# Attention outputs turned into rows by VectorE block transposes and a way through DRAM, and a changed entry into attention

## The chip, the cores and the metric

One core of a Trainium2 chip runs the kernel. The metric is the device time of one execution in microseconds. Of the kernel before, two runs were timed, 1617.72 and 1619.03 us, median 1618.38 us. A further execution was profiled.

## What is computed

The reference is one layer of a gated backbone over 1024 latent tokens and 256 context tokens, width 1024, all in float32. The normalised input goes through one wide projection into two branches, gated linear attention (GLA, four heads) and differential attention (eight heads of width 128), which are projected, gated, summed and projected again. The part around the change is differential attention and the first half of what follows it:

```python
a = jax.nn.softmax(s1, axis=-1) - lam * jax.nn.softmax(s2, axis=-1)
return jnp.einsum('bhqk,bhkv->bhqv', a.astype(v.dtype), v)
...
b = merge_heads(rms_norm(o_diff) * diff_gain * (1 - lam_init)) * jax.nn.silu(diff_gate)
y = jax.nn.sigmoid(m_gla) * (a @ w_br_gla) + jax.nn.sigmoid(m_diff) * (b @ w_br_diff)
```

The norm is over a token's 128 values in a head, so it needs the attention output with tokens along partitions. The product with w_br_diff contracts over those values and needs them along partitions again.

## The kernel before, in words

**Numbers and engines.** A float32 product is made of three float32r products of high and low parts. The high part is a rounding copy (ACT, or POOL from a copy), the low part a subtraction (DVE or POOL). TensorE (PE) also does all 128x128 transposes, by line 375; line 349 issues all other matmuls.

**Order.** The program is written by a scheduler in its own text. Tasks are Python generators. The class Driver (from line 59) keeps a modelled time for each engine and for the DMA queue, and resumes a task when what it yielded is due. `On(t, engine)` resumes it when that engine is about to come free, `AtPE(t)` when PE's modelled time reaches t, and any other time up to 1 us early (AHEAD, line 70). Of tasks due together, the one with the lowest `prio` number issues first. Each engine then runs its instructions strictly in the order in which they were issued, waiting on semaphores where the model was wrong. Driver.dma (lines 134 to 145) models a transfer: 0.45 us of issue on one shared queue, 0.6 us, the bytes at 360 GB/s, 1.8 us to the landing. All DMAs are issued by SP, one queue, in order: an issue that waits holds up all those behind it. `acq` and `rel` (lines 330 and 338) count the buffers of a tag; the table TAGS (line 235) gives each tag its pool and number.

**Stages.** Until about 900 us: projections, GLA. Then attention, 64 units (8 heads of 8 query tiles of 128). For a unit, PE makes two score rows of 1280 in the five PSUM banks of tile "s5", DVE takes maxima, ACT the exponentials, DVE the difference, PE ten transposes through the two "b1" banks, and ACT, POOL and DVE split them into "at". For a pair of units PE multiplies by the values into a "b1" bank (30 matmuls, `att_av`, line 2067). An order list (`att_order`, line 1914) fixes how scores, transposes and products of different units follow each other. Between them, `fill` (line 2193) puts independent matmuls into the one bank "mb": the rest of the gate projection, then the GLA output projection, 18 weight tiles in two halves each, with weights converted by `conv` (line 2210) from "raw" into "wt". From about 1458 us: the projection of attention's output in seven block products (`diff`), then the last projection.

**The pair's end**, `att_fin` (line 2142), runs once for each of 32 pairs (head hd, pair pr). It loads the gate values g (128 tokens x 2 x 128). ACT copies the product po to `ot`, whose 128 partitions are values and whose 256 columns are tokens. PE transposes its halves into pt, a "b1" bank (line 2160). ACT squares and sums each half, DVE multiplies pt by g, DVE and POOL make the inverse root, DVE scales into `oo`, PE transposes back into pb (line 2183), ACT copies that, and a DMA stores it in d_bT, from where `diff` loads it. The task holds one of two "fin" slots from before the products of `att_av` until the store is issued, and up to five "b1k" buffers are shared by such tasks.

**The entry.** GLA's last step for a head and group of 256 tokens is `post` (line 1795): it transposes the gated output through a PSUM tile "tp" (line 1816), splits it and stores it. `to_gla` (line 1277) waits for the last of them and closes GLA's PSUM pool with "gs", "go" and "gt"; `to_b` (line 2582) then waits for "mm" and "tp", closes their pool, opens the pools of "mb" and "s5" in that place and lets attention and fill begin. `half_tile` (line 2245) waits for its weight tile's event, which `conv` sets after one ACT copy and one DVE subtraction of 128x1024.

Of the kernel before, what the change touches and what calls it, by code (L numbers as in the profile page):

```python
# [20 lines left out]
P = 128  # L21
# [4 lines left out]
NK = D // P  # L26
# [206 lines left out]
class Hybrid:  # L233
# [6 lines left out]
        w=("sbA", 18), p=("sbA", 5), pl=("sbA", 4), rope=("sbA", 1),  # L240
# [6 lines left out]
        gsm=("sbA2", 8), gbi=("sbA2", 2), fresh=("sbA2", 1),  # L247

        wt=("sbW", 4), ft=("sbW", 2), aq=("sbG", 4), xa=("sbG", 4), vv=("sbB", 3),
        e5=("sbF", 6), at4=("sbB", 6), at2=("sbB", 2), ac=("sbB", 2), b1k=("sbB", 5), fin=(None, 2),  # L250

        ya=("sbC", 8), yb=("sbC", 8), yc=("sbD", 8), yf=("sbK", 8), yg=("sbG", 8), sf=("sbC", 2), o=("sbC", 4), wr=("sbD", 4), yd=("sbD", 4),

# [150 lines left out]
    def scratch(self):  # L404
        d = self.dram
        self.d_q = [d(f"d_q{h}", [P, S]) for h in range(4)]
        self.d_k = [d(f"d_k{h}", [P, T]) for h in range(4)]
        self.d_la = [[d(f"d_la{r}{h}", [P, T]) for h in range(4)] for r in range(2)]
        self.d_v = [d(f"d_v{c}", [T, 512]) for c in range(2)]
        self.d_gg = [d(f"d_gg{c}", [S, 512]) for c in range(2)]  # L410
        self.d_dg = [d(f"d_dg{c}", [S, 512]) for c in range(2)]
        self.d_dv = [[d(f"d_dv{j}{c}", [T, 512]) for c in range(2)] for j in range(2)]
        self.d_qT = [d(f"d_qT{c}", [4, P, 2, S]) for c in range(2)]
        self.d_kT = [[d(f"d_kT{j}{c}", [4, P, T]) for c in range(2)] for j in range(2)]
        self.d_aT = [[d(f"d_aT{j}{h}", [2, P, S]) for h in range(4)] for j in range(2)]
        self.d_bT = [d(f"d_bT{i}", [P, S]) for i in range(8)]
        self.d_m = [[d(f"d_m{j}{i}", [P, S]) for i in range(8)] for j in range(2)]
        self.d_pre = {n: d(f"d_pre_{n}", [P, 4, 512]) for n in ("w11", "w21", "w22", "t1", "t2", "t3", "t4")}
        self.ev_pre = {(n, kk): Event() for n in self.d_pre for kk in range(4)}
        self.ev_gbt = Event()  # L420
        self.d_ps = {n: d(f"d_ps_{n}", [4, P, 512]) for n in ("s1", "s2", "s3", "s4")}
        self.ev_ps = {(n, k): Event() for n in self.d_ps for k in range(4)}
        self.d_y = [d(f"d_y{i}", [P, S]) for i in range(8)]


# [1073 lines left out]
    def gla_head(self, h):  # L1499


        nc, d = self.nc, self.d
# [292 lines left out]
        def post(g, po):  # L1795

            r0 = (g - 1) * 256
            for x in range(2):
                yield self.ev_st["gg", h // 2, 2 * g - 2 + x]
            yield from self.acq("gp")  # L1800
            gt = self.t("gp", [P, 2, 256])
            self.dma(gt, self.d_gg[h // 2][r0:r0 + 256, cols].rearrange("(c p) e -> p c e", p=P))
            ss = self.t("sm", [P, 2])
            for x in range(2):
                en = self.act.activation(self.gj, po[:, x], AF.Square, accum_out=ss[:, x:x + 1])
            yield en
            self.pool.tensor_scalar(ss, ss, 1.0 / 256, EPS, ALU.mult, ALU.add)
            self.pool.tensor_tensor(ss, ss, self.nhalf[:, 0:2], ALU.pow)
            yield self.d.when(ss, gt)
            for x in range(2):  # L1810
                e = self.dve.scalar_tensor_tensor(gt[:, x], po[:, x], ss[:, x:x + 1], gt[:, x], ALU.mult, ALU.mult)
            self.rel("go", e)
            yield AtPE(e)
            yield from self.acq("tp")
            yield from self.acq("pl", 2)
            pt = self.t("tp", [P, 2, 2, P])
            for c in range(2):
                for x in range(2):
                    e = self.tr(pt[:, x, c], gt[:, c, x * P:(x + 1) * P])
            self.rel("gp", e)  # L1820
            yield e
            hi = self.t("pl", [P, 2, 2 * P], F32R)
            lo = self.t("pl", [P, 2, 2 * P], F32R)
            e = yield from self.split(pt.rearrange("p x c t -> p x (c t)"), hi, lo)
            self.rel("tp", e)
            self.store([(self.d_aT[j][h][:, :, r0:r0 + 256].rearrange("x p t -> p x t"), x) for j, x in
                        enumerate((hi, lo))], ("pl", 2))
            self.aT_left -= 1
            if self.aT_left == 0:
                d.set(self.ev_gla)  # L1830
# [311 lines left out]
    def att_fin(self, hd, pr, po, zs):  # L2142

        nc, d = self.nc, self.d
        yield from self.acq("b1k", 2)
        g = self.t("b1k", [P, 2, P])
        self.dma(g, self.d_dg[hd // 4][pr * 256:(pr + 1) * 256, (hd % 4) * P:(hd % 4 + 1) * P].rearrange(
            "(c p) e -> p c e", p=P))
        ot = self.t("b1k", [P, 256])
        e = self.act.activation(ot, po, AF.Copy)  # L2150
        self.rel(self.PO, e)
        z2 = self.t("sm", [P, 2])
        for x in range(2):
            self.dve.tensor_scalar(z2[:, x:x + 1], zs[x][:, 0:1], zs[x][:, 0:1], EPS, ALU.mult, ALU.mult)
        yield AtPE(e)
        yield from self.acq("b1k")
        yield from self.acq("b1")
        pt = self.t("b1", [P, 2, P])
        for x in range(2):
            e = self.tr(pt[:, x], ot[:, x * P:(x + 1) * P])  # L2160
        self.rel("b1k", e)
        yield On(e, "ACT")
# [4 lines left out]
        yield d.on("DVE", pt, g)  # L2167
        e2 = self.dve.tensor_tensor(g, pt, g, ALU.mult)
        self.rel("b1", max(e, e2))
        yield On(e, "DVE")  # L2170
        for x in range(2):
            self.dve.tensor_scalar(ss[:, x:x + 1], ss[:, x:x + 1], 1.0 / P, z2[:, x:x + 1], ALU.mult, ALU.add)
        yield d.on("POOL", ss)
        yield On(self.pool.tensor_tensor(ss, ss, self.nhalf[:, 0:2], ALU.pow), "DVE")
        for x in range(2):
            e = self.dve.tensor_scalar(oo[:, x], g[:, x], ss[:, x:x + 1], None, ALU.mult)
        self.rel("b1k", e)
        yield AtPE(e)
        yield from self.acq("b1k")
        yield from self.acq("b1")  # L2180
        pb = self.t("b1", [P, 2, P])
        for x in range(2):
            e = self.tr(pb[:, x], oo[:, x])
        self.rel("b1k", e)
        yield On(e, "ACT")
        bb = self.t("b1k", [P, 2, P])
        self.rel("b1", self.act.activation(bb, pb, AF.Copy))
        self.store([(self.d_bT[hd][:, pr * 256:(pr + 1) * 256], bb.rearrange("p x t -> p (x t)"))],
                   ("b1k", 1), ("fin", 1), ev=self.ev_bp[hd, pr])
        if (hd, pr) == (7, 3):  # L2190
            self.d.set(self.ev_att)

    def fill(self):


        d, a = self.d, self.a
        todo = [(0, s, self.win, C_MG + s * P) for s in range(self.fill_from, 16)] + \
               [(1, s, a["w_br_gla"][0], s * P) for s in range(8)]
        evs = [[Event()] for _ in todo]
        ws = {}  # L2200

        def load():
            for n, (kind, _, src, o) in enumerate(todo):
                yield from self.acq("raw")
                raw = self.t("raw", [P, NK, P])
                yield self.dma(raw, src[:, o:o + P].rearrange("(k p) c -> p k c", p=P))
                d.spawn(conv(n, raw), 0.0, prio=3)
            d.set(self.ev_loaded)

        def conv(n, raw):  # L2210
            yield self.ev_b2
            yield from self.acq("wt", 2)
            if n == len(todo) - 1:
                d.set(self.ev_conv)
            hi = self.t("wt", [P, NK, P], F32R)
            lo = self.t("wt", [P, NK, P], F32R)
            yield d.on("ACT", raw)
            self.act.activation(hi, raw, AF.Copy)
            yield d.on("DVE", hi)
            e = self.dve.tensor_tensor(lo, raw, hi.bitcast(F32), ALU.subtract)  # L2220
            self.rel("raw", e)
            ws[n] = (hi, lo)
            d.set(evs[n][0], e)

        yield self.wlast
        d.spawn(load(), prio=3)
        yield self.ev_b

# [381 lines left out]
    def phase_c(self):  # L2610
        a, d = self.a, self.d
# [3 lines left out]
        def to_c():  # L2615
# [10 lines left out]
            self.open("sbD")  # L2626
            d.set(self.ev_c1)
            yield self.ev_att
            yield from self.idle("b1", "b1k", "vv", "at4", "at2", "ac")
            self.close("psB1", "sbB")  # L2630
            self.open("sbC", "psD")
            d.set(self.ev_c2)
# [173 lines left out]
```

## Time and profile before

| | us |
|---|---|
| median of the two runs | 1618.38 |
| the profiled execution | 1616.59 |
| its span, first to last instruction | 1614.9 |
| DMA: share of 16 engines' time, queue of SP | 63.7% |
| ACT busy / DVE busy / POOL busy | 836.2 / 1223.5 / 634.2 |

The profile page gives busy time for each engine (PE matmuls, PEld weight loads, DVE = VectorE, ACT = ScalarE, POOL = GpSimd, SP = the queue of DMAs). Matmuls overlap in their pipeline, so a matmul's duration in the profile is longer than the time from its start to the next one's start; the second is its place in PE's row. Groups are named by tiles, out<-in. A wait is put down to the instruction that released it.

### The profile page before, as it was taken

To read this page: it belongs to the slowest core of one execution; us is meant where nothing else is said; L and a number is where in the kernel's file an instruction comes from. 1 tells how busy PE (TensorE), PEld (TensorE's weight loads), DVE (VectorE), ACT (ScalarE), POOL (GpSimd) and SP (SyncE) were. 2 spreads that over 40 slices of the span, in tenths; PEclk is the share of its full clock that TensorE was granted. 3 is DMA by queue.
4 is the path that set the end of the run, shared out by engine and by line. 5 is a ranking of instruction groups with operands and counts; after the bars stand their busy time and mean duration, and the time that the engine had idled before them with its cause. 6 is when DMAs were issued, how large, how long until landed. Compare 5 with 4: busy or idle time off the path is not lost.

```text
span 1614.9 us, 24351 instructions
## 1 busy us (share of the span) xinstructions
PE 1590.6 (98%) x8229; PEld 1328.0 (82%) x8229; DVE 1223.5 (76%) x2117; ACT 836.2 (52%) x1719; POOL 634.2 (39%) x663
## 2 busy tenths in 40 slices
PE   7999999999999999999999999999999999999999
PEld 3788888888888888888888788888888888888887
DVE  4787945576877779767677688878788888889994
ACT  4776523445343454655435466665665656656331
POOL 1500000001325667535464256656765666560000
PEclk9999999999999999999999999999999999999999
DMA  8576896998778467564645944545587555348662
GB/s 310 199 256 242 330 305 230 343 328 297 275 246 267 123 198 233 163 212 122 185 118 165 251 116 121 151 128 150 151 265 218 158 136 151 112 152 280 210 206 100
DMA packets 259565, 331.16 MB, mean 205 GB/s; under 512 B 22600, under 2 KB 160752, under 8 KB 259440
## 3 DMA queue, kind: packets, MB, share of 16 engines
q1 hardware_dynamic: 259440, 329.60, 63.7%
q8 instruction: 65, 1.06, 0.3%
q14 instruction: 60, 0.49, 0.1%
HBM read 225.20 MB, written 104.33 MB: 204 GB/s over the span
## 4 chain that ended last, share of the span: by engine, by line
PE 91%; DVE 4%; ACT 1%; DMA 1%; POOL 1%; issue 1%; SPq 0%; ACTq 0%; DVEq 0%; POOLq 0%
PE mm L349 31%; PE mb L349 11%; PE s L349 8%; PE mc L349 7%; PE b L349 6%; PE tp L349 6%; PE gt L349 5%; PE b L375 4%; PE gs L349 4%; PE go L349 4%; PE mz L349 2%; PE tp L375 2%; DVE sm L201 1%; POOL at L201 1%; DMA w<-in_w_ada 1%
## 5 line engine op out<-in xcount | busy, mean ns | idle before, releaser
L349 PE MATMUL mm<-w,h 128*128 128x512 f32 x912 | 231.0, 400 | 0.0
L349 PE MATMUL mb<-h,wt 128*128 128x512 f32 x840 | 222.8, 400 | 0.0
L201 DVE TENSOR_REDUCE sm<-s 128x1 f32<-128x1024 f32 (+1 forms) x192 | 193.3, 1037 | 16.4 <-PE s L349 9.9
L201 ACT ACTIVATE e<-s,sm 128x1280 f32<-128x1280 f32 x128 | 169.3, 1328 | 57.7 <-DVE sm L201 54.5
L349 PEld LDWEIGHTS mm<-w,h 128*128 128x128 f32 x912 | 167.4, 188 | 32.7
L201 POOL TENSOR_TENSOR at<-ac,at 128x512 fp32r<-128x512 f32 x128 | 186.6, 1458 | 10.7
L349 PEld LDWEIGHTS mb<-h,wt 128*128 128x128 f32 x840 | 151.4, 188 | 28.7 <-DVE ft L201 0.3
L201 POOL TENSOR_SCALAR at<-ac 128x512 fp32r<-128x512 f32 x128 | 98.4, 768 | 192.2 <-ACT ac L201 191.7
L349 PE MATMUL s<-hk,aq 128*128 128x512 f32 x744 | 169.2, 364 | 1.9 <-ACT e L201 1.8
L349 PE MATMUL mm<-h,w 128*128 128x512 f32 x672 | 168.2, 400 | 1.1 <-DVE h L201 1.1
L349 PEld LDWEIGHTS mm<-h,w 128*128 128x128 f32 x672 | 123.7, 188 | 26.5 <-DVE h L201 1.6
L201 DVE TENSOR_TENSOR w<-raw,w 128x512 fp32r<-128x512 f32 x128 | 95.7, 764 | 53.4 <-ACT w L201 51.2
L349 PEld LDWEIGHTS s<-hk,aq 128*128 128x128 f32 x744 | 117.6, 189 | 19.1 <-ACT e L201 4.3
L349 PE MATMUL b<-at,vv 128*128 128x256 f32 x960 | 130.1, 287 | 1.1 <-ACT ac L201 0.8
L349 PEld LDWEIGHTS b<-at,vv 128*128 128x128 f32 x960 | 119.5, 191 | 2.8 <-ACT ac L201 1.0
L201 ACT ACTIVATE w<-raw 128x512 fp32r<-128x512 f32 x128 | 78.1, 626 | 84.0 <-PE tp L349 23.8
L201 DVE SCALAR_TENSOR_TENSOR e<-e,sm,e 128x1280 f32<-128x1280 f32 x64 | 118.3, 1849 | 0.9
L201 ACT ACTIVATE ac<-b 128x512 f32<-128x512 f32 x122 | 72.4, 598 | 88.8 <-PE b L375 87.1
L201 POOL TENSOR_TENSOR sm<-sm,nhalf 128x2 f32<-128x2 f32 (+2 forms) x94 | 107.2, 1141 | 28.1 <-DVE sm L201 22.8
L349 PE MATMUL mm<-w,g 128*128 128x512 f32 x432 | 105.7, 389 | 0.0
L349 PEld LDWEIGHTS mm<-w,g 128*128 128x128 f32 x432 | 81.1, 188 | 16.8
L375 PE MATMUL b<-ident,e 128*128 128x128 f32 x610 | 92.6, 273 | 1.3 <-ACT ac L201 0.8
(353 smaller groups left out, 3050.8 us busy)
## 6 DMA issues: line engine op xcount, KB each, us to landing
raw<-in_w_in SPq DMA_DIRECT2D x62, 512.0 KB, 4.2
g<-d_s SPq DMA_DIRECT2D x32, 640.0 KB, 6.3
g<-d_s SPq DMA_DIRECT2D x32, 512.0 KB, 5.8
aq<-d_qT SPq DMA_DIRECT2D x124, 128.0 KB, 3.3
d_dv<-pl SPq DMA_DIRECT2D x40, 256.0 KB, 3.3
gv<-d_v SPq DMA_DIRECT2D x40, 256.0 KB, 3.2
d_kT<-pl SPq DMA_DIRECT2D x40, 256.0 KB, 2.7
hk<-d_kT SPq DMA_DIRECT2D x32, 320.0 KB, 5.7
```

What stands on the lines that cost most here:

```text
L201: self.ins = f(out, *args, **kw).ins
L349: self.ins = self.nc.tensor.matmul(out, lhsT, rhs, start=start, stop=stop, skip_group_check=more).ins
L375: self.nc.tensor.transpose(out, src, self.ident[:n, :n])
```

## The change

For all pairs but the last two (head 7, pairs 2 and 3, `late`), the way of `ot` into rows is another. DVE transposes each 32x32 block of `ot` into a new tile bt (tag "bt", two buffers). Four DMAs store bt, each from 32 partitions (8 pieces of 32 values, 128 bytes, in each), in a DRAM tensor d_ot of its own for each pair. After these, one DMA reads it back as pt with tokens along partitions (tag "bp", two buffers, pieces of 512 bytes). The two PE transposes and the "b1" bank of pt go. The multiplication by g on its own goes; the two scalings by the inverse root become operations that take pt, the root and g at once. The rest of the task is as it was.

At the entry, the last `post` of GLA uses the PSUM tile "gt" in place of "tp". The first weight tile of fill is converted at prio -5 instead of 3, in two halves, and its event is set after the first half.

```diff
+        self.d_ot = {(hd, pr): d(f"d_ot{hd}{pr}", [8, 32, P]) for hd in range(8) for pr in range(4)}
...
-            yield from self.acq("tp")
+            tg = "gt" if (h, g) == (3, 4) else "tp"
+            yield from self.acq(tg)
             yield from self.acq("pl", 2)
-            pt = self.t("tp", [P, 2, 2, P])
+            pt = self.t(tg, [P, 2, 2, P])
...
+        late = hd == 7 and pr > 1
+        if late:
...
+        else:
+            yield from self.acq("bt")
+            bt = self.t("bt", [P, 8, 32])
+            yield On(e, "DVE")
+            e = self.dve.transpose(bt.rearrange("p b c -> p (b c)"), ot)
+            self.rel("b1k", e)
+            dt = self.d_ot[hd, pr]
+            yield e
+            for i in range(4):
+                e = self.dma(dt[:, :, 32 * i:32 * i + 32].rearrange("b r c -> r b c"), bt[32 * i:32 * i + 32])
+            self.rel("bt", e)
+            yield e
+            yield from self.acq("bp")
+            yield from self.acq("b1k")
+            pt = self.t("bp", [P, 2, P])
+            yield On(self.dma(pt, dt.rearrange("(x j) r e -> (j r) x e", x=2)), "ACT")
...
-            e = self.dve.tensor_scalar(oo[:, x], g[:, x], ss[:, x:x + 1], None, ALU.mult)
+            if late:
+                e = self.dve.tensor_scalar(oo[:, x], g[:, x], ss[:, x:x + 1], None, ALU.mult)
+            else:
+                e = self.dve.scalar_tensor_tensor(oo[:, x], pt[:, x], ss[:, x:x + 1], g[:, x], ALU.mult, ALU.mult)
...
-                d.spawn(conv(n, raw), 0.0, prio=3)
+                d.spawn(conv(n, raw), 0.0, prio=3 if n else -5)
...
+            ws[n] = (hi, lo)
+            w = NK if n else NK // 2
+            for k in range(0, NK, w):
+                ks = slice(k, k + w)
+                yield d.on("ACT", raw)
+                self.act.activation(hi[:, ks], raw[:, ks], AF.Copy)
+                yield d.on("DVE", hi)
+                e = self.dve.tensor_tensor(lo[:, ks], raw[:, ks], hi[:, ks].bitcast(F32), ALU.subtract)
+                if k == 0:
+                    d.set(evs[n][0], e)
```

More of the change, by code (lines that the diff above doesn't have):

```diff
@@ L249 @@
         wt=("sbW", 4), ft=("sbW", 2), aq=("sbG", 4), xa=("sbG", 4), vv=("sbB", 3),
-        e5=("sbF", 6), at4=("sbB", 6), at2=("sbB", 2), ac=("sbB", 2), b1k=("sbB", 5), fin=(None, 2),
+        e5=("sbF", 6), at4=("sbB", 6), at2=("sbB", 2), ac=("sbB", 2), b1k=("sbB", 5), bt=("sbB", 2), bp=("sbB", 2), fin=(None, 2),
         ya=("sbC", 8), yb=("sbC", 8), yc=("sbD", 8), yf=("sbK", 8), yg=("sbG", 8), sf=("sbC", 2), o=("sbC", 4), wr=("sbD", 4), yd=("sbD", 4),
@@ L1824, in post @@
             e = yield from self.split(pt.rearrange("p x c t -> p x (c t)"), hi, lo)
-            self.rel("tp", e)
+            self.rel(tg, e)
             self.store([(self.d_aT[j][h][:, :, r0:r0 + 256].rearrange("x p t -> p x t"), x) for j, x in
@@ L2154, in att_fin @@
             self.dve.tensor_scalar(z2[:, x:x + 1], zs[x][:, 0:1], zs[x][:, 0:1], EPS, ALU.mult, ALU.mult)
[L2155 to L2162, printed above, removed]
+        late = hd == 7 and pr > 1
+        if late:
+            yield AtPE(e)
+            yield from self.acq("b1k")
+            yield from self.acq("b1")
+            pt = self.t("b1", [P, 2, P])
+            for x in range(2):
+                e = self.tr(pt[:, x], ot[:, x * P:(x + 1) * P])
+            self.rel("b1k", e)
+            yield On(e, "ACT")
+        else:
[3 more added lines that the diff above has]
+            e = self.dve.transpose(bt.rearrange("p b c -> p (b c)"), ot)
+            self.rel("b1k", e)
+            dt = self.d_ot[hd, pr]
[5 more added lines that the diff above has]
+            yield from self.acq("bp")
+            yield from self.acq("b1k")
+            pt = self.t("bp", [P, 2, P])
+            yield On(self.dma(pt, dt.rearrange("(x j) r e -> (j r) x e", x=2)), "ACT")
         oo = self.t("b1k", [P, 2, P])
@@ L2166, in att_fin @@
             e = self.act.activation(oo[:, x], pt[:, x], AF.Square, accum_out=ss[:, x:x + 1])
-        yield d.on("DVE", pt, g)
-        e2 = self.dve.tensor_tensor(g, pt, g, ALU.mult)
-        self.rel("b1", max(e, e2))
+        if late:
+            yield d.on("DVE", pt, g)
+            e2 = self.dve.tensor_tensor(g, pt, g, ALU.mult)
+            self.rel("b1", max(e, e2))
         yield On(e, "DVE")
@@ L2175, in att_fin @@
         for x in range(2):
-            e = self.dve.tensor_scalar(oo[:, x], g[:, x], ss[:, x:x + 1], None, ALU.mult)
+            if late:
+                e = self.dve.tensor_scalar(oo[:, x], g[:, x], ss[:, x:x + 1], None, ALU.mult)
+            else:
+                e = self.dve.scalar_tensor_tensor(oo[:, x], pt[:, x], ss[:, x:x + 1], g[:, x], ALU.mult, ALU.mult)
         self.rel("b1k", e)
+        if not late:
+            self.rel("bp", e)
         yield AtPE(e)
@@ L2216, in conv @@
             lo = self.t("wt", [P, NK, P], F32R)
[L2217 to L2220, printed above, removed]
+            ws[n] = (hi, lo)
[8 more added lines that the diff above has]
+                    d.set(evs[n][0], e)
             self.rel("raw", e)
-            ws[n] = (hi, lo)
-            d.set(evs[n][0], e)
         yield self.wlast
@@ L2628, in to_c @@
             yield self.ev_att
-            yield from self.idle("b1", "b1k", "vv", "at4", "at2", "ac")
+            yield from self.idle("b1", "b1k", "bt", "bp", "vv", "at4", "at2", "ac")
             self.close("psB1", "sbB")
```

## The prediction

> **What bounds the kernel now.** I read the page first: its totals and its slices.
>
> ```profile
> span 1614.9 us, 24351 instructions
> PE 1590.6 (98%) x8229; PEld 1328.0 (82%) x8229; DVE 1223.5 (76%) x2117; ACT 836.2 (52%) x1719; POOL 634.2 (39%) x663
> PE   7999999999999999999999999999999999999999
> PEclk9999999999999999999999999999999999999999
> ```
>
> PE is busy in every slice at full granted clock, so an instruction taken off PE is worth its place in PE's row. Next, the stretch that the change works in (from the second pair's loads to the last pairs of attention), and what PE waited for there.
>
> ```profile
> 925.00:1430.00 505.00, 500.37 (x3068) 435.00 (x3068) 420.25 (x777) 308.23 (x629) 317.53 (x282) 1.00 0.53 153
> ...
> PE s L349 <- ACT e L201: 1.1, 2, 0.7
> PE b L375 <- DVE b1k L201: 1.1, 3, 0.4
> PE b L375 <- ACT ac L201: 0.8, 1, 0.8
> PE b L349 <- ACT ac L201: 0.8, 1, 0.8
> PE b L375 <- DVE at L201: 0.3, 1, 0.3
> ```
>
> The first row gives busy time of PE, weight loads, DVE, ACT, POOL. In 505 us PE idles 4.6 us; DVE is next at 420 (83%). No DMA is among PE's releasers. So the gain can only be PE instructions, and the danger is a new wait that reaches PE.
>
> **The change, part by part.**
>
> *Two transposes fewer on PE, for 30 of 32 pairs.* I read their price from starts in PE's timeline, not from durations.
>
> ```profile
> 1040.83 1.09 PE L349 MATMUL s<-hk,aq 128*128 128x512 f32 x4
> 1041.76 0.85 PE L349 MATMUL mb<-h,wt 128*128 128x512 f32 x3
> ...
> 1043.15 0.38 PE L375 MATMUL b<-ident,b1k 128*128 128x128 f32 x2
> 1043.28 1.19 PE L349 MATMUL s<-hk,aq 128*128 128x512 f32 x4
> 1044.30 0.85 PE L349 MATMUL mb<-h,wt 128*128 128x512 f32 x3
> ...
> 1057.96 1.53 PE L349 MATMUL mb<-h,wt 128*128 128x512 f32 x6
> 1059.33 0.60 PE L375 MATMUL b<-ident,b1k 128*128 128x128 f32 x4
> 1059.68 1.64 PE L349 MATMUL mb<-h,wt 128*128 128x512 f32 x6
> 1061.15 0.38 PE L375 MATMUL b<-ident,e 128*128 128x128 f32 x2
> ```
>
> Two transposes hold PE from 1043.15 to 1043.28, 0.13 us, and the four matmuls behind them take 1.02 us where four without take 0.93: 0.22 in all. Four take 0.35, and the six behind them 1.47 instead of 1.37: 0.45, or 0.225 for two. 30 x 0.225 = 6.75 us less. The other transpose pair of each task (line 2183) stays.
>
> *The entry.* What ends the wait of the first scores:
>
> ```profile
> 897.42 0.60 PE L375 MATMUL tp<-ident,gp 128*128 128x128 f32 x4
> 899.49 2.59 PE L349 MATMUL s<-hk,raw 128*128 128x512 f32 x12 [1.46 <-DVE pl L201]
> 901.92 5.61 PE L349 MATMUL mb<-h,wt 128*128 128x512 f32 x24
> ...
> 896.94 1.28 ACT L201 ACTIVATE p<-mm 128x512 f32<-128x512 f32 x2 [1.79 <-PE mm L349]
> ...
> 898.74 0.69 DVE L201 TENSOR_TENSOR pl<-tp,pl 128x512 fp32r<-128x512 f32 x1 [1.62 <-ACT pl L201]
> 899.68 1.23 DVE L201 TENSOR_TENSOR wt<-raw,wt 128x1024 fp32r<-128x1024 f32 x1 [0.25 <-ACT wt L201]
> ```
>
> The score tile takes the place of "mm" and "tp", and PE waits 1.46 us until DVE has read the last "tp". With that tile in "gt", what is late next is ACT's read of "mm", done at 898.22: scores could start at 898.3, a gain of 1.2 us. If the score tile's last bank is that of "gt", nothing is gained: 0 to 1.46, I take 1.2, as the next releaser is in view. Then the first fill matmul comes at 900.7, before DVE ends its weights at 900.91; the split into halves brings the first four blocks some 0.6 us earlier, so this costs nothing.
>
> *DVE and ACT.* The rows of the task's tiles:
>
> ```profile
> L201 ACT ACTIVATE b1k<-b x128: 269/354/421, 936.6 to 1466.3; 128x256 f32<-128x256 f32 x64, 128x128 f32<-128x128 f32 x64
> L375 PE MATMUL b<-ident,b1k x128: 270/272/331, 937.4 to 1466.0; 128*128 128x128 f32 x128
> L201 DVE TENSOR_SCALAR b1k<-b1k,sm x64: 273/286/1333, 943.4 to 1465.4; 128x128 f32<-128x128 f32 x64
> L314 SPq DMA_DIRECT2D b1k<-d_dg x32: 370/554/2155, 926.0 to 1455.6; - x32
> L201 DVE TENSOR_TENSOR b1k<-b,b1k x32: 405/414/418, 941.1 to 1460.4; 128x256 f32<-128x256 f32 x32
> ...
> DMA to landing us min/median/max: 1.7/3.3/7.0
> ```
>
> Per task DVE loses one TENSOR_TENSOR (0.414) and two TENSOR_SCALAR (0.286 each), 0.99 us, and gains a 32x32 transpose of 128x256 and two scalar_tensor_tensor of 128x128. No row shows such a transpose: I bound it by 0.29 and by the 1.23 of the 128x1024 operation above, and take 0.42, the row of the same size. The other two I take at 0.30. That is 1.02 for 0.99: no change (at the upper end 24 us more in 505, DVE at 88%). The transpose waits on DVE for ACT's copy, as the TENSOR_TENSOR waited for PE. ACT's squares read SBUF instead of PSUM, at the same size. The freed "b1" bank could save up to the 3.0 us that PE waited above for banks and copies; I take 0, since fill fills such gaps.
>
> *Five DMAs more per task, and a wait on two queues.* All go through SP. A store of 32 partitions has 256 pieces, as many as the 0.554 us issue of the "d_dg" load.
>
> ```profile
> hk<-d_kT SPq DMA_DIRECT2D x32, 320.0 KB, 5.7
> ...
> b1k<-d_dg SPq DMA_DIRECT2D x32, 128.0 KB, 3.6
> d_bT<-b1k SPq DMA_DIRECT2D x32, 128.0 KB, 2.9
> ...
> ACT b1k L201 <- PE b L375: 41.1, 41, 2.0
> ```
>
> The way through DRAM: three issues (1.66), the last store to its landing 2.9, the read to its landing 3.6: 8.2 us. The scheduler written into the kernel (lines 134 to 146) counts 4.3 for the stores and 3.2 for the read, 7.5, and puts the squares on ACT up to 1 us before that. So ACT stands 1.7 us instead of the 1.0 (41.1/41) of now before this task's reads: 30 x 0.7 = 21 us, with exponentials, copies and splits queued behind. Nothing to all of it can reach PE: 0 to 21 us. ACT is busy 308 of 505 us and PE waited for ACT 2.7 us in all while ACT itself waited 41 us at this place: I take a tenth, 2 us.
>
> On SP the read waits for the stores, about 2.4 us, and K, Q and gate loads and all stores stand behind it. The tight ones are the K loads at a head's end:
>
> ```profile
> 1089.99 1.24 SPq L314 DMA_DIRECT2D hk<-d_kT  x2
> ...
> 1099.64 1.54 PE L349 MATMUL s<-hk,aq 128*128 128x512 f32 x8
> ```
>
> The second is issued at 1090.6, lands 5.7 later at 1096.3, and the next head's scores start at 1099.64: 3.3 us to spare. Four issues and the wait (4.6 us) just ahead of it would cost PE 1.3 us; at seven heads 0 to 9 us. Pairs follow each other by 16.7 us (33.38 from 1036.72 to 1070.10 for two, rows below), so the block falls there in 4.6 of 16.7: at most 0.28 x 9 = 2.5, half of that on the mean of its places, and I take 1 us.
>
> **The sum.** The profiled execution took 1616.6 us. 1616.6 - 6.75 - 1.2 + 2 + 1 = 1611.65. The median of the runs shown, 1618.4, lies 1.8 above it: I forecast 1613.
>
> **The rivals.**
>
> *The waits eat the gain.* ACT passes on 40% of the 21 us, or half of it with the pair's second transposes late behind it: +8 to +10, 1619 to 1621. For it: those transposes are released by DVE's last step and already waited (1.1 us above). Against: DVE and POOL queues lie between.
>
> *The way outlasts the pair's two slots* (other side). A task holds one of two "fin" slots from its products to its last copy; the products two pairs on need the slot.
>
> ```profile
> 1036.72 2.40 PE L349 MATMUL b<-at,vv 128*128 128x256 f32 x18
> ...
> 1041.57 0.39 ACT L201 ACTIVATE b1k<-b 128x256 f32<-128x256 f32 x1
> ...
> 1043.56 0.28 ACT L201 ACTIVATE b1k<-b 128x128 f32<-128x128 f32 x1 [0.31 <-PE b L375]
> ...
> 1060.26 0.38 ACT L201 ACTIVATE b1k<-b 128x256 f32<-128x256 f32 x1
> ...
> 1070.10 2.32 PE L349 MATMUL b<-at,vv 128*128 128x256 f32 x18
> ```
>
> The copy ends at 1060.64, the products that need the slot start at 1070.10: 9.4 us to spare, with 1.6 us now from copy to squares. A way of up to 11 us is free; each us beyond costs half a us per pair, 15 us over 30. From 13.7 us on the kernel is over 32 us slower than before: 1651 and more. The forecast's 8.2 speaks against it; two longest landings of 7.0 in each task would make 15.7.
> The Trainium skill's page "VectorE: DVE Perf Modes", section "The three transpose paths", speaks against such a way: a plain copy that transposes by strides is 19 times slower than the DMA crossbar's 1309 ns for 128x128 bf16, an estimate of 25 us, with which this rival would hold. Its condition is a large innermost stride, and here 32 floats stay together; no run so far shows this copy.
>
> *PE pays whole durations for a transpose*, 0.272 us (the median in the rows of the task's tiles). Then 60 x 0.272 = 16.3 goes, and the time is 1603. The starts 0.13 us apart speak against it.
> The Trainium skill, "TensorE: Matmul & The Clock Gate", section "Part 4: PE-mode transpose", prices one at about 275 ns in a kernel, which by its rule would be an estimate of 16.5 us for the sixty; the trace agrees on the duration and not on the place it takes.
>
> *The entry does not do what it is for*: the scores still wait for that tile's bank. 1614.5.
>
> *K loads late at every head*: 9 instead of 1 and ACT's share doubled: 1623 to 1626.
>
> **How the numbers follow.** Forecast (1609 to 1616 by its own ends) 0.55; waits eat the gain 0.2; entry without effect 0.1; whole durations 0.05; K loads 0.05; slots outlasted 0.05. The range 1606 to 1626 leaves out the whole durations below and the slots above, 0.1 in all, and as much again for what no row bounds. A measurement of this kernel can tell about 2% (32 us) from no change: only the slots reach over it, and not always: slower 0.04, faster 0.01, same 0.95.
>
> **What would show it.** Right: 68 instead of 128 transposes from "b1k", PE busy down by some 10 (modelled durations) and its row denser by 6 to 7; first scores near 898.3; squares on ACT released by the DMA of the read, about 1.7 us each; landings of the stores near 2.9. Wrong: PE's waits on "s" and "b" for ACT or DVE well above 6 us in sum; any PE wait released by a K load; products released by a "fin" slot, seen as pairs further apart than 16.7 us; a DVE transpose far over 0.42 us.

## The result and the profile after

The changed kernel takes 1673.72 us (two runs, 1671.93 and 1675.51), the kernel before 1618.38: ratio 1.0339, 95% interval 1.0322 to 1.0356, 55 us slower. The forecast was 1613 us. The profiled execution took 1671.93 us. The page's totals, PE's slices and the granted clock:

```profile
span 1669.7 us, 24457 instructions
PE 1605.6 (96%) x8169; PEld 1330.5 (80%) x8169; DVE 1232.5 (74%) x2118; ACT 840.7 (50%) x1720; POOL 642.3 (38%) x663
PE   7999999999999999999999999899999999877999
...
PEclk9999999999999999999999999999999999988999
```

PE has 60 matmuls fewer (8169 for 8229), is busy 15 us longer, and is no longer full towards the end of attention. The same stretch as before, and the stretch in which attention ends here:

```profile
925.00:1430.00 505.00, 481.79 (x2845) 413.11 (x2844) 391.48 (x703) 284.94 (x571) 299.21 (x258) 0.99 0.59 164
...
1440.00:1506.00 66.00, 52.22 (x297) 43.13 (x296) 45.24 (x87) 34.45 (x80) 41.56 (x37) 0.87 0.31 88
```

In the first row's 505 us PE idles 23 us instead of 4.6 and issues 2845 matmuls instead of 3068. What it waited for in that stretch:

```profile
PE mb L349 <- ACT ft L201: 5.3, 5, 2.2
PE b L375 <- DVE b1k L201: 5.1, 5, 2.4
PE mb L349 <- DVE ft L201: 5.0, 3, 2.3
PE s L349 <- ACT e L201: 4.6, 5, 1.9
PE b L375 <- ACT ac L201: 2.9, 4, 1.0
```

No single releaser stands out, and none is a DMA. Read alone, these rows would send one after ACT and DVE; the experiments show that this is the wrong place. From the first pair's products to the last pair's, PE's row grew from 517.3 to 573.7 us:

```profile
932.40:1449.70 517.30, 512.31 (x3151) 445.71 (x3149) 431.79 (x795) 315.26 (x653) 333.11 (x295) 1.00 0.53 154
```

```profile
932.80:1506.50 573.70, 536.72 (x3159) 458.73 (x3158) 440.62 (x796) 319.47 (x651) 340.87 (x295) 0.98 0.55 153
```

The first row is of before, the second of after. The whole loss passes in this stretch: it is 56.4 us longer, and behind it 163.2 us follow instead of 165.2. Of the 56.4 us, 32.0 are idle (37.0 for 5.0) and 24.4 are time in which PE counts as busy. Of these 24.4, some 12 are the lower clock (0.98 over 573.7 us). Some 10 more are, by an estimate, another make-up of the work: the stretch holds 3159 matmuls for 3151, but 69 more of 128x512 (1313 for 1244; 0.227 us each in the 24 from 901.92 to 907.37 before) and 60 transposes fewer (0.10 us each, measured below). So part of the projection that came behind the last pair before now stands ahead of it.

The task that the prediction followed before (products at 1036.72), here from its products at 1046.82, in one timeline of PE, ACT, DVE and SP:

```profile
1046.82 2.40 PE L349 MATMUL b<-at,vv 128*128 128x256 f32 x18
...
1051.78 0.38 ACT L201 ACTIVATE b1k<-b 128x256 f32<-128x256 f32 x1
...
1057.80 0.43 DVE L201 STREAM_TRANSPOSE bt<-b1k 128x256 f32<-128x256 f32 x1
...
1061.06 1.88 SPq L314 DMA_DIRECT2D d_ot<-bt  x4
...
1064.88 0.46 SPq L314 DMA_DIRECT2D bp<-d_ot  x1
...
1068.62 0.31 ACT L201 ACTIVATE b1k<-bp 128x128 f32<-128x128 f32 x1 [1.37 <-DMA bp<-d_ot]
...
1084.38 0.38 ACT L201 ACTIVATE b1k<-b 128x256 f32<-128x256 f32 x1
...
1087.24 0.99 PE L349 MATMUL b<-at,vv 128*128 128x256 f32 x7
```

The copy ends at 1052.16 and the squares start at 1068.62: a way of 16.5 us, where it was 1.6 (1041.96 to 1043.56) and where the prediction said 8.2. 5.6 us of it pass before VectorE, busy with reductions and the 128x1280 operations, comes to the transpose, which takes 0.43; 2.8 until SP comes to the stores; 3.8 from the first store to the read; 3.7 from the read to the squares. The second copy ends at 1084.76, and the products that need this slot follow at 1087.24: the 9.4 us to spare are 2.5. Over the 30 pairs the median from the end of the products to the squares is 15.1 us (2.5 before), of it 5.3 until the transpose, 0.5 until the first store, 4.6 until the read and 3.4 until the squares, each the median of its own step (such rows of all pairs, first products at 932.8, last of the thirty at 1470.4). From its first products to the issue of its store a task took 16.4 us at the median and 27.4 at most before, 28.3 and 48.8 now. Two slots at a pair each 16.7 us give each task 33.4; no task of before passes that, and 9 of 30 do now.

### The profile page after: what moved, and what is told of

Same layout as the page of the kernel before. It is cut to its first block, busy times and chain, and to the rows that moved or that the text cites. A ratio compares the mean times of both kernels' runs of the same rounds, so it can differ in the third digit from the quotient of the medians.

```text
span 1669.7 us, 24457 instructions
## 1 busy us (share of the span) xinstructions
PE 1605.6 (96%) x8169; PEld 1330.5 (80%) x8169; DVE 1232.5 (74%) x2118; ACT 840.7 (50%) x1720; POOL 642.3 (38%) x663
## 4 chain that ended last, share of the span: by engine, by line
PE 80%; DVE 8%; issue 4%; DMA 3%; ACT 3%; POOL 2%; SPq 1%; DVEq 0%; ACTq 0%; POOLq 0%
PE mm L349 29%; PE mb L349 10%; PE mc L349 6%; PE s L349 6%; PE tp L349 5%; PE b L349 4%; PE gt L349 4%; PE go L349 4%; PE gs L349 4%; DVE sm L201 4%; PE b L375 3%; PE tp L375 2%; PE mz L349 2%; DVE e L201 1%; ACT e L201 1%
## 5 line engine op out<-in xcount | busy, mean ns | idle before, releaser
L349 PE MATMUL mb<-h,wt 128*128 128x512 f32 x888 | 233.8, 401 | 10.4 <-ACT ft L201 5.3
L201 POOL TENSOR_TENSOR at<-ac,at 128x512 fp32r<-128x512 f32 x128 | 197.9, 1546 | 10.7
L349 PEld LDWEIGHTS mb<-h,wt 128*128 128x128 f32 x888 | 160.4, 189 | 42.7 <-ACT ft L201 7.0
L201 POOL TENSOR_SCALAR at<-ac 128x512 fp32r<-128x512 f32 x128 | 104.0, 812 | 232.6 <-ACT ac L201 200.3
L349 PE MATMUL s<-hk,aq 128*128 128x512 f32 x744 | 173.4, 367 | 11.4 <-ACT e L201 11.3
L201 DVE SCALAR_TENSOR_TENSOR e<-e,sm,e 128x1280 f32<-128x1280 f32 x64 | 114.7, 1792 | 0.8
```

What stands on the lines that cost most here:

```text
L201: self.ins = f(out, *args, **kw).ins
L349: self.ins = self.nc.tensor.matmul(out, lhsT, rhs, start=start, stop=stop, skip_group_check=more).ins
```

## The experiments

Each ratio is to the kernel before, run on the same chip.

### Is the gain there: entry and transposes

**The entry alone**, all pairs with the old way:

```diff
-        late = hd == 7 and pr > 1
+        late = True
```

> The kernel before with the changed entry alone (all 32 pairs take the PE transposes). My sum: 1.2 us less, 1617 us, and the first scores start right behind ACT's read of mm. If the score tile still waits for the bank of gt: 1618 us. If the entry has a part in the loss: above 1625 us.

Measured: 1616.96 us, ratio 0.9988 (0.9978 to 0.9997).

```profile
900.46 0.60 PE L375 MATMUL gt<-ident,gp 128*128 128x128 f32 x4
901.31 2.58 PE L349 MATMUL s<-hk,raw 128*128 128x512 f32 x12 [0.25 <-ACT p L201]
```

The first scores start 0.85 us behind the transposes instead of 2.07, released by ACT's read of "mm": 1.22 us, as forecast. (Everything ahead of the entry varies by up to 4.7 us between executions, so only distances are compared.)

**The first transposes issued twice** in the kernel before, the second unknown to the scheduler, so that the order stays:

```diff
+            self.nc.tensor.transpose(pt[:, x], ot[:, x * P:(x + 1) * P], self.ident)
             e = self.tr(pt[:, x], ot[:, x * P:(x + 1) * P])
```

> The kernel before with each of the first transposes of all 32 pairs issued twice, unknown to the scheduler, so that the order of all else stays: 64 transposes more on PE. Price by place in PE's row: 64 x 0.109 = 7 us more, 1625 to 1628 us. If PE had idle time to give there: less than 3 us more. By whole durations: 17 us more.

Measured: 1624.75 us, ratio 1.0040 (1.0027 to 1.0052): 6.5 us for 64, 0.10 us each. That is the place in PE's row read from starts (0.11), not the duration of 0.272.

**The transposes not issued, in the same order** (the scheduler still counts them; their readers read `ot`):

```diff
-            e = self.tr(pt[:, x], ot[:, x * P:(x + 1) * P])
+            e = self.d.op("PE", 0.109, [pt[:, x]], [ot[:, x * P:(x + 1) * P]])
...
```

> The kernel before without the first two transposes of all 32 pairs, the squares and gates reading the copied product (values of other tokens), while the scheduler still counts the transposes and their bank, so that the order of all else stays. If the order took the gain back in the run without them (1.000): 5 to 8 us less here, ratio 0.995 to 0.997. If PE is not the limit at these places: no change.

Measured: 1615.09 us, ratio 0.9981 (0.9972 to 0.9990): 3.1 us gained, less than the 5 to 8 expected.

**The same, with the scheduler knowing it**, so that it makes another order:

```diff
-        yield AtPE(e)
-        yield from self.acq("b1k")
-        yield from self.acq("b1")
-        pt = self.t("b1", [P, 2, P])
-        for x in range(2):
-            e = self.tr(pt[:, x], ot[:, x * P:(x + 1) * P])
-        self.rel("b1k", e)
+        pt = ot.rearrange("p (x t) -> p x t", x=2)
...
```

> The kernel before without the first two PE transposes of all 32 pairs; squares and gates read the copied product itself, so the output is of untransposed values. Nothing is put in their place: what 64 transposes are worth on PE. My price: 64 x 0.11 = 7 us less, 1611 to 1613 us. If the order of the rest matters more than PE's work: 1616 us or more.

Measured: 1619.97 us, ratio 1.0000 (0.9991 to 1.0010). So the 6.75 us that the prediction took off PE are there when transposes are added to a fixed order, half there when they are taken out of it, and gone when the order is made anew. No run here shows more than a few us to be won by taking them off PE.

### The slots

**Three slots instead of two** in the changed kernel:

```diff
-        ... bt=("sbB", 2), bp=("sbB", 2), fin=(None, 2),
+        ... bt=("sbB", 2), bp=("sbB", 2), fin=(None, 3),
```

> The changed kernel with three fin slots in place of two, nothing else (the five b1k buffers stay). Slots theory: the products of a pair wait for a task two pairs back, so the third slot gives most of the 55 us back: 1612 to 1630 us, pairs 16 to 17 us apart again, fill lasting to the last pairs. Late-landing theory (ACT stands on the read's landing and passes it on to PE): the landings are as late as before, so 1660 us or more.

Measured: 1645.47 us, ratio 1.0153 (1.0135 to 1.0171): 28 us less than with two, between what the two theories expected. In its trace 11 of 30 pairs start their products before the task two pairs back has issued its store, by up to 16.6 us; in the changed kernel, whose two slots forbid it, none does.

**Three slots in the kernel before**, the same edit:

> The kernel before, with three fin slots instead of two; nothing else. Theory (the change's tasks outlast two slots, those of before do not): a pair of before holds its slot 16.4 us at the median (from its first product to the issue of its store), well inside the 33 us that two slots give at a pair each 16.7 us, so the third slot changes nothing: 1615 to 1621 us. Rival (a third slot is worth something to any order, and the 28 us that it gave back to the changed kernel are no sign of the slots' shortage there): 1595 to 1610 us.

Measured: 1625.33 us, ratio 1.0044 (1.0027 to 1.0061). A third slot is worth nothing to tasks that fit into two; it even made an order 7 us worse, which the text did not expect.

**One slot in the kernel before** (`fin=(None, 1)`):

> The kernel before with one fin slot in place of two; no DRAM way, no transposes on VectorE. Slots theory: a task that outlasts its slots is enough by itself, with the same signs as the changed kernel: 1640 to 1690 us, PE idle 30 us or more above the kernel before, fill used up before the last pairs. Late-landing theory: without new DMAs little changes, 1618 to 1630 us, as fill covers the gaps.

Measured: 1661.65 us, ratio 1.0263 (1.0246 to 1.0280).

**Each slot of the kernel before held 15 us longer**, the task itself unchanged:

```diff
-                   ("b1k", 1), ("fin", 1), ev=self.ev_bp[hd, pr])
+                   ("b1k", 1), ev=self.ev_bp[hd, pr])
+        self.rel("fin", AtPE(d.now + 15.0))
```

> The kernel before, but each fin slot is given back by the scheduler 15 us after the last copy; engines and DMAs do the same work. That is about what the changed kernel's tasks last longer. Slots theory: 9 to 18 us were to spare, so part of the pairs wait: 1625 to 1645 us, between the kernel before and the one with one slot (1662). Late-landing theory: no change, 1618 to 1622 us.

Measured: 1634.34 us, ratio 1.0095 (1.0078 to 1.0112), 15 us. By the rival's own price, 15 us for each us beyond 9.4 to spare, it would have been 84. That price was taken from one of the tighter pairs; half of them have 16 us and more to spare. So slots alone, with nothing late on the chip, slow this kernel down, though by far less than that price.

### The way itself

**Without the way through DRAM** in the changed kernel: stores and read left out, and the scheduler knows it. Squares and scalings read bt where it stands, so the values are those of other tokens.

```diff
-            for i in range(4):
-                e = self.dma(dt[:, :, 32 * i:32 * i + 32].rearrange("b r c -> r b c"), bt[32 * i:32 * i + 32])
-            self.rel("bt", e)
...
-            pt = self.t("bp", [P, 2, P])
-            yield On(self.dma(pt, dt.rearrange("(x j) r e -> (j r) x e", x=2)), "ACT")
+            pt = bt.rearrange("p (x b) c -> p x (b c)", x=2)
+            yield On(e, "ACT")
...
```

> The changed kernel with the VectorE transpose, but the squares and scalings read the transposed blocks themselves: the four stores and the read through DRAM are left out, so the rows are not put together (values of other tokens stand in them). Slots theory: some 6 to 8 us of the task's life go, it fits two slots nearly always: 1608 to 1622 us. If instead the transpose's place on VectorE were the cause (DVE theory), it stays above 1645 us.

Measured: 1626.89 us, ratio 1.0046 (1.0031 to 1.0061). 47 of the 55 us go with the way, though 1626.89 is above the 1608 to 1622 of the slots theory: the VectorE transpose alone still gains nothing.

**Three slots, and the scheduler counts the read's landing 4 us later**, so that it puts the squares later into ACT's queue:

```diff
-            yield On(self.dma(pt, dt.rearrange("(x j) r e -> (j r) x e", x=2)), "ACT")
+            e = self.dma(pt, dt.rearrange("(x j) r e -> (j r) x e", x=2)) + 4.0
+            d.ready[d.key(pt)] = e
+            yield On(e, "ACT")
```

> Three fin slots, and the scheduler counts 4 us more for the read, so that squares and what hangs on them are put later on ACT, DVE, POOL and PE; no transfer changes. In the run with three slots ACT stood 38.7 us on the read's landing and PE idled about 25 us more than before. If those 25 us are the late landings passed on: ACT's standing falls below 12 us and the time to 1612 to 1630 us. If they come from the third slot's order or from VectorE: about 1645 us as before.

Measured: 1620.18 us, ratio 1.0001 (0.9992 to 1.0011): 25 us less than with three slots alone.

**The same with 2 us:**

> Three slots, and the scheduler counts 2 us more for the read instead of 4. If the order alone decides by a few us: 1612 to 1625 us, ACT standing on the landing between 5 and 20 us. If it beats the kernel before, this is the change's better form: ratio 0.994 to 0.998.

Measured: 1625.92 us, ratio 1.0046 (1.0033 to 1.0059), just above the range, with one wait of ACT for the read, 1.5 us.

**The same 4 us with two slots:**

> The same 4 us on the changed kernel with its two slots. Slots theory: each task holds its slot 4 us longer, half of which per pair is lost: 25 to 60 us more, 1690 to 1735 us, though ACT stands less. Late-landing theory: less standing is a gain, as with three slots: 1645 to 1665 us. The two runs together tell the theories apart by their signs.

Measured: 1697.58 us, ratio 1.0486 (1.0470 to 1.0501). One edit, 25 us better with three slots and 24 us worse with two: with two slots, a longer life of the tasks costs more than what it was spent for wins. What the 4 us mend with three slots is seen in the version without them, whose wait of ACT for the read stands in the first row:

```profile
ACT b1k L201 <- DMA bp<-d_ot: 38.7, 18, 8.1
```

Its longest, in the timelines of SP, DVE, ACT and PE:

```profile
1235.77 10.36 SPq L314 DMA_DIRECT2D h<-d_aT  x14
...
1243.62 0.43 DVE L201 STREAM_TRANSPOSE bt<-b1k 128x256 f32<-128x256 f32 x1
...
1252.23 2.09 SPq L314 DMA_DIRECT2D d_ot<-bt  x4
...
1254.92 2.65 SPq L314 DMA_DIRECT2D aq<-d_qT  x4
1257.67 0.53 SPq L314 DMA_DIRECT2D bp<-d_ot  x1
...
1262.09 0.31 ACT L201 ACTIVATE b1k<-bp 128x128 f32<-128x128 f32 x1 [8.07 <-DMA bp<-d_ot]
...
1263.59 1.54 PE L375 MATMUL b<-ident,e 128*128 128x128 f32 x6 [6.19 <-ACT ac L201]
```

Fourteen loads of GLA's output take SP 10.4 us; the transpose has ended at 1244.05, but its stores, behind these loads and what was issued after them, come at 1252.23 and the read at 1257.67; ACT stands 8.07 us in front of the squares, and PE loses 6.19 us, because the copy "ac" is queued behind the squares. In the version with 4 us more no wait of ACT for the read is recorded at all.

### Two misses

**The transpose not queued for VectorE**: asked for when ACT's copy is due, not when VectorE is about to come free. Meant to shorten the life of a task.

```diff
-            yield On(e, "DVE")
+            yield e
             e = self.dve.transpose(bt.rearrange("p b c -> p (b c)"), ot)
```

> The changed kernel with two slots; the VectorE transpose is issued as soon as the copy is due, and not only when VectorE is about to come free. Slots theory: the task's life shortens by what the transpose waited (0.5 to 11 us, mostly 5), so about half of the slots' 28 us and perhaps some late landings go: 1630 to 1655 us. If that wait has no part: 1665 us or more.

Measured: 1666.01 us, ratio 1.0297 (1.0283 to 1.0311), above the theory's range and where the text put a wait that has no part. The wait for the transpose fell to 2.6 us at the median, but from first products to store a task still took 27.0 us instead of 28.3, and ACT's wait for the read rose, from the changed kernel's first row to this version's second:

```profile
ACT b1k L201 <- DMA bp<-d_ot: 24.3, 13, 6.3
```

```profile
ACT b1k L201 <- DMA bp<-d_ot: 41.6, 17, 6.8
```

So little of a task's life was saved, and landings came later than counted more often.

**The same edit with three slots and 4 us:**

> The changed kernel with three slots, the scheduler counting the read's landing 4 us later, and the VectorE transpose asked for when ScalarE's copy is due instead of when VectorE is about to come free. Theory: with slots and late landings both out of the way nothing of the way through DRAM is left to be gained, so a transpose some 3 us earlier is worth nothing: 1616 to 1623 us, no different from the version without this edit (1620.2). Rival (the queueing of the transpose, not slots and landings, still holds back the gain of the transposes taken off PE): 1610 to 1615 us, below the kernel before.

Measured: 1649.42 us, ratio 1.0190 (1.0172 to 1.0208). Neither theory had that. ACT waited once for the read, 3.2 us, so little of the way was late, and still 29 us were lost. So an order made by the scheduler can lose that much by itself, and the split that I held until then (half the loss from slots, half from late landings), which rested on versions with different orders, was not safe.

### The order kept, the DMAs taken out

The next four runs keep the order of four versions on PE, ACT, DVE and POOL instruction for instruction. The scheduler counts stores and read as it did; they are only not issued, and the readers read bt (values of other tokens). What goes is what these DMAs cost on the chip, by landing late or by holding SP; what remains lies in the order, or in the rest of the work.

```diff
-                e = self.dma(dt[:, :, 32 * i:32 * i + 32].rearrange("b r c -> r b c"), bt[32 * i:32 * i + 32])
+                e = d.dma(4 * 32 * 256, dt, bt)
...
-            pt = self.t("bp", [P, 2, P])
-            yield On(self.dma(pt, dt.rearrange("(x j) r e -> (j r) x e", x=2)), "ACT")
+            pt = bt.rearrange("p (x b) c -> p x (b c)", x=2)
+            yield On(d.dma(4 * P * 256, pt, dt), "ACT")
...
```

The order of the changed kernel:

> The changed kernel with the order of its instructions on PE, ACT, DVE and POOL unchanged: the scheduler still counts the four stores and the read of each pair, but they are not issued, and the squares and scalings read the transposed tile bt where it stands (so values of other tokens; the way through DRAM is left out). What the chip does later than the scheduler counts on the way is gone; what two slots do to the order stays. Theory (of the 55 us some 28 come from slots, fixed in the order, and some 25 from landings that come later than counted): 1645 to 1653 us. Rival A (all of it is in the order): 1666 to 1674 us. Rival B (all of it is lateness on the chip, and the third slot helped only by giving late landings room): 1614 to 1626 us.

The order of the changed kernel with three slots:

> The order of the changed kernel with three slots (1645.5 us), with stores and reads counted but not issued. Theory (what is left with three slots are landings later than counted): 1616 to 1624 us. Rival (what is left is the order that the scheduler makes, and counting 4 us more helped by making another one): 1640 to 1646 us.

The order with three slots and 4 us:

> The order of the version with three slots and later squares (1620.2 us), with stores and reads counted but not issued. Theory (its order already has the landings in time, nothing of the way costs any more): 1616 to 1620 us. Rival (the way still costs some 6 us there, the price of the transposes taken off PE): 1610 to 1614 us.

The order with three slots, 4 us and the transpose not queued:

> The order of the version with three slots, later squares and the transpose not queued (1649.4 us), with stores and reads counted but not issued, as in the run above. That version showed no wait of ScalarE for the read among its largest, and still lost 29 us against the same version with the transpose queued. Theory (its loss is in the order that the scheduler makes, not in lateness of the way): 1643 to 1650 us. Rival (lateness of the way, through VectorE or the queue of DMAs): 1614 to 1626 us.

Measured, in the order of these texts: 1667.17, 1624.63, 1619.68 and 1645.20 us. The first is rival A, the second lies just above its theory's range, the others within theirs.

| order of | with the way | DMAs not issued | in the order, us | late on the chip, us |
|---|---|---|---|---|
| the changed kernel | 1.0339 (1.0322 to 1.0356) | 1.0297 (1.0281 to 1.0312) | 48 | 7 |
| with three slots | 1.0153 (1.0135 to 1.0171) | 1.0034 (1.0021 to 1.0047) | 6 | 19 |
| three slots, 4 us | 1.0001 (0.9992 to 1.0011) | 1.0005 (0.9995 to 1.0014) | 1 | none |
| three slots, 4 us, not queued | 1.0190 (1.0172 to 1.0208) | 1.0159 (1.0144 to 1.0174) | 26 | 5 |

(us: the ratio in the third column, and the difference of the two, times 1618.) The first row settles the question against my split: of the 55 us 48 stay in the order, and only 3 to 10 go when every landing is early. That the 48 are the order's, and not the rest of the work's, shows in the second row: both versions without the DMAs run the same instructions on PE, ACT, DVE and POOL (8169, 1720, 2118 and 663, alike in every shape); only the number of slots and the order made with it differ. All three versions with two slots and the way lose 48 us or more (1.0297 to 1.0486), all four with three slots 31 us or less (1.0001 to 1.0190). Three slots take away the order's loss, and only then do late landings come to the fore, with 19 us, which counting the landing later takes away. The last row is the miss: its loss is in the order too, and what in that order costs 26 us was not followed further.

Why the order is slow with two slots is seen where a task lives longest. In the changed kernel, timelines of PE, DVE, SP and ACT:

```profile
1173.15 2.40 PE L349 MATMUL b<-at,vv 128*128 128x256 f32 x18
...
1180.19 0.43 DVE L201 STREAM_TRANSPOSE bt<-b1k 128x256 f32<-128x256 f32 x1
...
1182.14 2.93 SPq L314 DMA_DIRECT2D d_ot<-bt  x4
...
1188.65 9.11 SPq L314 DMA_DIRECT2D h<-d_aT  x14
...
1198.75 0.37 SPq L314 DMA_DIRECT2D bp<-d_ot  x1
...
1209.59 0.33 ACT L201 ACTIVATE b1k<-bp 128x128 f32<-128x128 f32 x1
...
1221.94 0.32 SPq L314 DMA_DIRECT2D d_bT<-b1k  x1
...
1225.68 2.32 PE L349 MATMUL b<-at,vv 128*128 128x256 f32 x18
```

and in the same order without the DMAs, PE alone:

```profile
1194.82 2.19 PE L349 MATMUL b<-at,vv 128*128 128x256 f32 x17
1196.85 0.86 PE L349 MATMUL mb<-h,wt 128*128 128x512 f32 x3
...
1202.31 2.33 PE L349 MATMUL mb<-h,wt 128*128 128x512 f32 x9
...
1208.18 1.17 PE L349 MATMUL mb<-h,wt 128*128 128x512 f32 x3
...
1212.19 5.03 PE L349 MATMUL mb<-h,wt 128*128 128x512 f32 x21
1218.65 1.66 PE L349 MATMUL mb<-h,wt 128*128 128x512 f32 x6 [1.43 <-DVE ft L201]
1220.28 0.94 PE L349 MATMUL mb<-h,wt 128*128 128x512 f32 x3
1221.19 3.67 PE L349 MATMUL mb<-h,wt 128*128 128x512 f32 x15
1224.70 2.31 PE L349 MATMUL b<-at,vv 128*128 128x256 f32 x18
```

The task holds its slot from 1173.15 to 1221.94, 48.8 us; its read stands behind 14 loads on SP, which the scheduler counts too. The next pair has the other slot. The pair after that starts 30.0 us behind it (1195.64 to 1225.68), and just as far in the run without DMAs (1194.82 to 1224.70): the order has it so, and early data do not help. PE hardly stands meanwhile (it idles 3.2 us): it gets 60 fill matmuls, where a pair of before has 24 as a rule (the 3, 9, 3, 21, 6, 3 and 15 of the rows). That is why no large wait shows in PE's rows. But that fill is missing at the end: from the pair at 1439.1 on none is left between pairs, they follow by 12 to 24 us all the same, and PE idles 13.8 of the 66 us of the row 1440.00 to 1506.00.

## Why the prediction was wrong, point by point

**The step that failed is the price of the way through DRAM, 8.2 us.** It was the sum of issues and landings, all of which were right or too high: the last store lands in 1.7 us (2.9 taken), the read in 2.8 (3.6 taken), an issue takes 0.44 (0.55 taken).

```profile
L314 SPq DMA_DIRECT2D d_ot<-bt x120: 303/444/1747, 937.9 to 1488.7; - x120
L201 DVE STREAM_TRANSPOSE bt<-b1k x30: 426/433/447, 937.5 to 1486.9; 128x256 f32<-128x256 f32 x30
...
DMA to landing us min/median/max: 1.5/1.7/6.7
```

What it left out are the transpose itself (0.43 us) and the queues in front of each step: VectorE ahead of the transpose (5.3 us at the median), SP ahead of stores and read, ACT ahead of the squares. With them the way is 13.9 us at the median, from the end of the copy to the squares. It had been said that a way of more than 11 us outlasts the slots and that each us beyond costs 15: 3 us beyond give 45, and the order's share is 48. So the rival with a chance of 0.05 was the mechanism. That its price came near is luck as far as these runs show, for it is no law: held 15 us longer, the slot cost 15 and not 84. The prediction weighed the rival by its own sum of 8.2 us; the wait for VectorE, 83% busy, was in view and was never put into that sum.

**ACT standing for the landing, 1.7 us per task and a tenth of it to PE: wrong, but not the cause here.** The squares' wait before the change was read rightly, 1.0 us at a time (23 waits from 925 to 1430 us):

```profile
L201 ACT ACTIVATE b1k<-b 128x128 f32<-128x128 f32 x58 | 15.6, 276 | 23.5 <-PE b L375 23.4
```

But it was to grow by 21 us to 51, and it hardly grew: 24.3 us in 13 of 30 tasks. In the other 17 the read had landed when ACT came to the squares. All lateness on the chip together cost 7 us against the 3 of the sum. With three slots the share is much higher: 38.7 us of standing, 19 us late on the chip.

**Sixty transposes less, 6.75 us: right as a price, wrong as a gain.** The doubled transposes cost 0.10 us each; made anew, the order took the whole gain back. The Trainium skill's page "TensorE: Matmul & The Clock Gate", section "Part 4: PE-mode transpose", gives about 275 ns for a transpose in one kernel, which matches the duration of 272 ns; the doubled run shows that its place in PE's row costs 0.10 us.

**The entry, 1.2 us: right** (1.22).

**VectorE's work, no change: right in its parts.** The transpose takes 0.433 us (0.42 taken), the scalings 0.350 (0.30 taken).

**K loads, 1 us: nothing of it is seen.** No wait of PE for a K load is among the rows of the changed kernel.

**Landings of such pieces.** The Trainium skill's page "VectorE: DVE Perf Modes", section "The three transpose paths", was cited with a copy that transposes by strides, an estimate of 25 us. The trace shows no such time for this copy, in which 32 floats stay together: pieces of 128 bytes land in 1.7 us at the median.

What stays open: why a life that is longer by 12 us at the median costs 48 us, when a slot held 15 us longer cost 15 (there the task itself, its buffers and its reads stayed as early as before); and what in an order costs a few us up to 26 where no slot is short (three slots before the change, +7; the way left out, +7; the transpose not queued, +26).

## What to carry to other kernels

When a step becomes a round trip, price it from one buffer's or slot's acquisition to its release, with the wait in every in-order queue it passes, and set it against slots times pace. Where a program orders itself by modelled times, a run with the order kept and one cost taken out tells what the order loses from what the chip loses; waits in the profile do not, because such an order hides a shortage by spending filler work early. And two shortages can need both their mends: 1673.7 us, 1645.5 with the third slot, 1697.6 with the later squares, 1620.2 with both.

## What the runs showed of the hardware

The granted clock fell where PE had many short waits: 0.87 from 1440 to 1506 us in the changed kernel (0.50 from 1479.4 to 1492.9 and 1.00 just before and behind), though the longest waits there are these:

```profile
PE s L349 <- ACT e L201: 5.3, 3, 2.9
PE mc L349 <- DVE aq L201: 4.1, 2, 2.2
```

Before, with PE full, it was 1.00 in the same stretch:

```profile
1440.00:1506.00 66.00, 65.28 (x318) 54.76 (x318) 54.92 (x103) 37.73 (x78) 10.54 (x10) 1.00 0.79 267
```

The Trainium skill's page "TensorE: Matmul & The Clock Gate" says in its section "A second HAM failure mode: psum-queue depth-cycling" that frequent short idles also bring the clock down; the trace agrees, with no wait over 2.9 us. So an idle us cost more than itself here: with 32.0 us more idle from the first pair's products to the last's came a clock of 0.98, some 12 us more. Over the whole execution the clock of 0.989 makes some 18 us.

SP's time to issue is a resource of its own: 14 loads hold it 9.1 to 10.4 us, 0.65 to 0.74 us each, and whatever is issued behind them waits, whether its data are there or not.
